# A hybrid decoder block on one core: the first transfers in another order and on other queues, and two output tiles that take the last merge tile's share at their end

## The chip, the cores and the metric

The kernel runs on one core of a Trainium2 chip. It is one launch of one program; the time is the device time of that core in microseconds (us), and the number that stands for a kernel is the median of its runs. All arithmetic is in float32: a factor that goes through the matrix engine is split into a high part (stored as fp32r) and a low part (what the high part leaves), and a product takes three matmuls: high by high, high by low, low by high.

## The reference

One layer over 512 positions and 1024 channels; eight heads of 64 in two key groups; a feed-forward width of 2816:

```python
h = rmsnorm(x, norm1_g)
a_b, a_c, a_x, q, kc, vc, ksl, vsl, kwn, vwn, g_nsa, g_merge = split(h @ w_in)
y_a = a_b * causal_dwconv(a_c * a_x, conv_a_w)
y_b = nsa(rope(rmsnorm(q)), k_cmp, v_cmp, k_sel, v_sel, k_win, v_win, sigmoid(g_nsa))
gm  = sigmoid(g_merge)
mix = gm[:, :D] * (y_a @ w_a_out) + gm[:, D:] * (y_b @ w_b_out)
x   = x + mix @ w_o
h   = rmsnorm(x, norm2_g)
gu  = h @ w_ffn_in
g   = causal_dwconv(gu[:, :D_FF], ffn_conv_w) + ffn_conv_b
x   = x + (silu(g) * gu[:, D_FF:]) @ w_ffn_out
```

## The kernel before, in words

Everything is held with channels on the 128 partitions, in KD = 8 channel tiles of 512 positions. The program is written stage by stage, but the order in which an engine gets its instructions is not the order of the text: a list scheduler with a simulated timeline places them (the context is opened with `schedule_with_timeline_sim=True`), so an edit in one place can move instructions in another. Each engine then works its own list strictly in order.

**The start.** `tok_round(0, first_slot)` makes the first projection: for each of eight channel tiles k, four position tiles (banks `pj_s`, three times, and `pj_o`) take three matmuls of 384 columns each: `xg_h` by `wh`, `xg_l` by `wh`, `xg_h` by `wl`. That is 12 matmuls per k and 96 in the round. `first_slot` is called for pairs of channel tiles, j = 0 to 3 (k = 0 and 1, 2 and 3, and so on). It issues the transfers (`par`, a table of 116 columns with the norm gains; `xT`, the input, into `x_all`; `w_tok`, the weights, into `wr_t`), then has ScalarE scale the input by the gain (L262, `xg_h`; VectorE makes `xg_l`, L263), split the weights (`split`, L152 and L153) and square the input for the norm's sums (L291). `chain(ops)` fixes the order of these on ScalarE. Ahead of it `NWU` = 11 matmuls on a tile of ones (`wu`, L183) keep the matrix engine busy while the first data arrive.

**The merge.** After the attention, the convolution branch and the gates, eight merge tiles are made, two per turn (L771 to L784): the matrix engine makes `pmb`, VectorE multiplies by the gate (L780), GpSimd adds the other branch (L781, `t_all`), ScalarE takes the high part (`mix_h`, L782), VectorE the low part (`mix_l`, L783).

**The output projection.** For the eight output tiles in `O_ORDER` = (0, 4, 1, 5, 2, 6, 3, 7): a weight tile is loaded (`ring_w`: raw tile, then high and low parts in rings of three), `dense` makes 24 matmuls into a bank `po` (16 with the high weights, 8 with the low ones; each pair of units needs one of the eight merge tiles, the last of them `mix_h[7]`, `mix_l[7]`), VectorE adds the input (L814), ScalarE makes `xv` and a square (L818, `sq`/`sqb`, L823), and after each second tile `x_forms` makes seven combinations of two halves (`xv`, L803 to L805) whose high and low parts `xf_h`, `xf_l` (L152 and L153, one step of 1792 columns per pair) feed the feed-forward part. All eight `po` banks come from the pool `d_bank`, which has two; `s_bank` has three, and the attention scores before and the feed-forward products `p45` and `p37` after it use that.

**The first feed-forward pair.** The products of pair 0 are written in two parts (`late`, L926 to L937): first three of the four channel units of every product (L931), then the last one (L937), since the last unit waits for the output projection's last pair. Between them stand the matmuls `pr_n` of the second norm's sums (L375).

Of the kernel before, what the change touches and what calls it, by code (L numbers as in the profile page):

```python
# [14 lines left out]
AF = mybir.ActivationFunctionType  # L15
# [5 lines left out]
S = 512  # L21
KD = D // P
# [23 lines left out]
NRAW = 4  # L46
NWF = 3
NE = 3
NWU = 11
QT_ORDER = (3, 2, 1, 0)  # L50
NPT = 3
NF_T = 10
# [30 lines left out]
def tile_block(ctx: ExitStack, tc: tile.TileContext, xT, pos, par, par2, w_tok, w_a3, w_gate, w_ao, w_bo, w_o,  # L83
               w_ff, w_dn, c_w1, out):
    nc = tc.nc
# [22 lines left out]
    def bank(tag, name, bufs):  # L108
        return ps.tile([P, 512], F32, name=name, tag=tag, bufs=bufs)

    def d_bank(name):
        return bank("d", name, 2)
# [53 lines left out]
    def raw_tile(name):  # L166
        return wf.tile([P, D], F32, name=f"wr_{name}", tag="wr", bufs=NRAW)

    def ring_w(src, name):
        raw = raw_tile(name)  # L170
        nc.sync.dma_start(raw, src)
        h, l = ring(name)
        split(h, l, raw)
        return h, l


    ones = const([P, P], "ones")
    nc.gpsimd.memset(ones, 1.0)
    warm = const([P, 2], "warm")
    nc.gpsimd.memset(warm[:, 1:2], 0.0)  # L180
    wu = d_bank("wu")
    for i in range(NWU):
        nc.tensor.matmul(wu[:, 0:P], ones, ones, start=True, stop=True)  # L183
    par_sb = const([P, NPAR], "par")
# [28 lines left out]
    def behind(later, earlier):  # L213

        tc.add_manual_dep(later.ins, earlier.ins.name,
                          mybir.DependencyInfo(mybir.DependencyClass.NoSync, mybir.DependencyReason.DATA),
                          reason="order")
# [51 lines left out]
    def first_slot(j, raw, hi, lo):  # L269
        a, b = CH[0]  # L270
        xr = x_all[:, 2 * j:2 * j + 2]
        if j == 0:
            nc.scalar.dma_start(par_sb, par)
            for k in range(2):
                nc.sync.dma_start(xr[:, k], xT[:, k])
                d = (nc.sync if k else nc.scalar).dma_start(raw[:, k], w_tok[k, :, a:b])
                if k == 0:

                    behind(nc.scalar.activation(warm[:, 0:1], ones[:, 0:1], AF.Copy), d)
            x0 = scale_x(0, xr[:, 0], (slice(0, S // 2), slice(S // 2, S)))  # L280
            w0 = split(hi[:, 0], lo[:, 0], raw[:, 0])
            x1 = scale_x(1, xr[:, 1], (slice(0, S),))
            w1 = split(hi[:, 1], lo[:, 1], raw[:, 1])
            ops = [x0[0], w0, x0[1]] + x1 + [w1]
        else:
            nc.sync.dma_start(xr, xT[:, 2 * j:2 * j + 2])
            nc.sync.dma_start(raw, w_tok[2 * j:2 * j + 2, :, a:b].rearrange("k p n -> p k n"))
            ops = [scale_x(2 * j + k, xr[:, k], (slice(0, S),))[0] for k in range(2)]
            ops.append(split(hi, lo, raw))
        sq = w_tmp(f"sq{j}", (2, S))  # L290
        ops.append(nc.scalar.activation(sq, xr, AF.Square))  # L291

        chain(ops)
        if j == 0:
            sq_sum.append(sq)
        else:
            nc.vector.tensor_add(sq_sum[0], sq_sum[0], sq)
# [102 lines left out]
    def dense(acc, units, first=True, last=True):  # L400

        for i, (wh, wl, xh, xl) in enumerate(units):
            nc.tensor.matmul(acc, wh, xh, start=first and i == 0, stop=False)  # L403
            nc.tensor.matmul(acc, wh, xl, start=False, stop=False)  # L404
        for i, (wh, wl, xh, xl) in enumerate(units):
            nc.tensor.matmul(acc, wl, xh, start=False, stop=last and i == len(units) - 1)  # L406

    def w_units(w, xh, xl, nk, k0=0, koff=0):
        wh, wl = w
        return [(wh[:, (koff + k) * P:(koff + k + 1) * P], wl[:, (koff + k) * P:(koff + k + 1) * P],  # L410
                 xh[:, k0 + k, :], xl[:, k0 + k, :]) for k in range(nk)]
# [357 lines left out]
    mix_h = const([P, KD, S], "mix_h", F32R, pc)  # L769
    mix_l = const([P, KD, S], "mix_l", F32R, pc)  # L770
    for i in range(4):  # L771
# [3 lines left out]
        w = ring_w(w_bo[i], f"bo{i}")  # L775
        for n, j in enumerate((2 * i, 2 * i + 1)):
            acc = t_bank(f"pmb{j}")
# [13 lines left out]
    x1 = const([P, KD, S], "x1", F32, px)  # L791
    O_ORDER = (0, 4, 1, 5, 2, 6, 3, 7)
# [13 lines left out]
        split(xf_h[:, k], xf_l[:, k], v)  # L806

    sq2 = sb.tile([P, S], F32, name="sq2", tag="rb")
    for n, j in enumerate(O_ORDER):
        w = ring_w(w_o[j], f"o{j}")  # L810
        acc = d_bank(f"po_{j}")
        dense(acc, w_units(w, mix_h, mix_l, KD))
        xj = x1[:, j, :]
        nc.vector.tensor_add(xj, xj, acc)  # L814
        k, half = j % 4, j // 4
        if half == 0:
            v = pc.tile([P, 7, TH], F32, name=f"xv{k}", tag="xv", bufs=2)
        nc.scalar.activation(v[:, 2 * half:2 * half + 2].rearrange("p a t -> p (a t)"), xj, AF.Copy,  # L818
                             scale=par_sb[:, G2 + j:G2 + j + 1])
        if half == 1:  # L820
            x_forms(k, v)
        sq = sq2 if n == 0 else pc.tile([P, S], F32, name=f"sqb{j}", tag="tb", bufs=2)
        nc.scalar.activation(sq, xj, AF.Square)  # L823
        if 0 < n < KD - 1:
            nc.vector.tensor_add(sq2, sq2, sq)
# [246 lines left out]
```

## Time and profile before

| what | value |
|---|---|
| median of the runs | 720.97 us |
| lowest run | 720.72 us |
| the profiled execution: its time, and its span from first to last instruction | 719.79 us, 718.1 us |
| matrix engine (PE) busy | 711.1 us, 99% of the span |
| VectorE (DVE), ScalarE (ACT), GpSimd (POOL) busy | 532.5, 437.7, 183.3 us |
| first matmul of the first projection | 6.36 us |
| the wait ahead of the output projection's last unit | 1.3 us |

How to read it: PE is the row of matmuls, PEld that of the weight loads that go beside them, and a name followed by q (SPq, ACTq, POOLq) is that engine's instruction queue issuing a transfer. A timeline row gives the start, the time taken, the engine, the line, the operation with the tiles it writes and reads, and in brackets how long the engine had been idle before it and what ended that. The buffer numbers are left out of the tiles' names. A row with a count, x2 or x8, is several instructions that follow each other, and its time is that of all. Matmuls are pipelined: a matmul's duration is longer than its distance to the next, and the distance is what counts.

### The profile page before, as it was taken

Reading aid. Unit: us, or ns where it says so; the run is one execution under the profiler, and the core shown is the slowest. Engines: PE = TensorE matmul, PEld = TensorE weight load, DVE = VectorE, ACT = ScalarE, POOL = GpSimd, SP = SyncE. Lnnn points to the kernel's source line nnn. Section 1 sums busy time; section 2 is a strip of 40 time slices with the busy share of each in tenths; the row PEclk is TensorE's granted clock in tenths of the full one; section 3 lists DMA queues with packets and bytes.
Section 4 is the critical chain, followed back from the end, with each engine's and each line's share of the span. In section 5 each row is a group of like instructions: output and inputs, shape, how many; then the busy total and the mean of one; then the engine's idle time right before and its main releaser. Section 6 shows DMA issues by size and latency. Waiting matters only on the chain.

```text
span 718.1 us, 11433 instructions
## 1 busy us (share of the span) xinstructions
PE 711.1 (99%) x4309; PEld 635.5 (89%) x4309; DVE 532.5 (74%) x973; ACT 437.7 (61%) x738; POOL 183.3 (26%) x176
## 2 busy tenths in 40 slices
PE   9999999999999999999999999999999999999997
PEld 8999888888888888887889999899999999999986
DVE  6887885677568676465695899997787877878643
ACT  7535655877667767443585776676564766646430
POOL 3151422133433333435011211221211222111110
PEclk9999999999999999999999999999999999999999
DMA  7333677511111221062676798987878778785575
GB/s 272 98 94 118 177 175 175 120 60 58 60 60 60 77 70 60 1 234 70 223 191 135 164 230 210 226 202 186 201 187 220 172 184 202 187 205 104 120 140 151
DMA packets 41143, 105.48 MB, mean 147 GB/s; under 512 B 3968, under 2 KB 9216, under 8 KB 41088
## 3 DMA queue, kind: packets, MB, share of 16 engines
q1 hardware_dynamic: 26528, 70.41, 29.8%
q0 software_dynamic: 14272, 34.08, 27.4%
q8 instruction: 34, 0.56, 0.3%
q10 hardware_dynamic: 288, 0.26, 0.1%
q14 instruction: 21, 0.17, 0.1%
HBM read 102.64 MB, written 2.10 MB: 146 GB/s over the span
## 4 chain that ended last, share of the span: by engine, by line
PE 96%; POOL 1%; DVE 1%; ACT 1%; DMA 1%; issue 0%; ACTq 0%
PE p L404 9%; PE p L406 9%; PE p L403 9%; PE pdn L404 6%; PE pdn L403 6%; PE pdn L406 6%; PE pg L403 4%; PE pg L404 4%; PE pg L406 4%; PE pa L403 3%; PE pa L406 3%; PE pa L404 3%; PE pt L650 2%; PE po L406 2%; PE po L403 2%; PE po L404 2%
## 5 line engine op out<-in xcount | busy, mean ns | idle before, releaser
L404 PE MATMUL p<-xf_l,sh 128*128 128x256 f32 x336 | 80.6, 277 | 0.0
L403 PE MATMUL p<-xf_h,sh 128*128 128x256 f32 x336 | 80.6, 277 | 0.0
L152 ACT ACTIVATE sh<-s 128x1024 fp32r<-128x1024 f32 x44 | 46.2, 1057 | 38.2 <-PE p L404 24.5
L404 PE MATMUL pdn<-al,wh_d 128*128 128x512 f32 x176 | 68.8, 391 | 0.0
L403 PE MATMUL pdn<-ah,wh_d 128*128 128x512 f32 x176 | 68.6, 391 | 0.0
L404 PEld LDWEIGHTS p<-xf_l,sh 128*128 128x128 f32 x336 | 63.0, 188 | 0.1
L403 PEld LDWEIGHTS p<-xf_h,sh 128*128 128x128 f32 x336 | 63.0, 188 | 0.1
L160 POOL DMA_DIRECT2D wl_s<-in_w_ff_dram x22 | 19.5, 885 | 167.6 <-ACT wl_s L159 156.1
L153 DVE TENSOR_TENSOR sl<-s,sh 128x1024 fp32r<-128x1024 f32 x44 | 53.8, 1225 | 8.7 <-ACT sh L152 8.7
L158 ACT ACTIVATE wh_s<-wr_s 128x1024 fp32r<-128x1024 f32 x22 | 23.3, 1057 | 53.5 <-PE pdn L404 50.1
L135 POOL TENSOR_TENSOR wl_g<-wr_g,wh_g 128x1024 fp32r<-128x1024 f32 x16 | 38.4, 2402 | 64.4 <-ACT wh_g L133 31.1
L406 PE MATMUL p<-xf_h,sl 128*128 128x256 f32 x336 | 51.6, 277 | 0.0
L403 PE MATMUL pg<-xg_h,wh_g 128*128 128x512 f32 x128 | 51.0, 398 | 0.0
L404 PE MATMUL pg<-xg_l,wh_g 128*128 128x512 f32 x128 | 50.7, 396 | 0.0
L406 PE MATMUL pdn<-ah,wl_d 128*128 128x512 f32 x176 | 47.7, 389 | 0.0
L160 POOL DMA_DIRECT2D wl_d<-in_w_dn_dram x22 | 26.5, 1203 | 77.6 <-ACT wl_d L159 70.4
L991 DVE TENSOR_TENSOR x<-x,pdn 128x512 f32<-128x512 f32 x48 | 33.1, 690 | 16.2 <-PE pdn L406 15.5
L406 PEld LDWEIGHTS p<-xf_h,sl 128*128 128x128 f32 x336 | 44.5, 188 | 0.2
L403 PE MATMUL p<-xf_h,wh_s 128*128 128x256 f32 x168 | 40.5, 277 | 0.0
L404 PE MATMUL p<-xf_l,wh_s 128*128 128x256 f32 x168 | 40.5, 277 | 0.0
L406 PEld LDWEIGHTS pdn<-ah,wl_d 128*128 128x128 f32 x176 | 33.0, 188 | 6.8
L404 PEld LDWEIGHTS pdn<-al,wh_d 128*128 128x128 f32 x176 | 33.1, 188 | 6.2
(348 smaller groups left out, 2138.4 us busy)
## 6 DMA issues: line engine op xcount, KB each, us to landing
wr_s<-in_w_ff_dram SPq DMA_DIRECT2D x44, 512.0 KB, 5.1
wl_s<-in_w_ff_dram POOLq DMA_DIRECT2D x22, 512.0 KB, 7.6
wr_d<-in_w_dn_dram SPq DMA_DIRECT2D x22, 512.0 KB, 6.5
wl_d<-in_w_dn_dram POOLq DMA_DIRECT2D x22, 512.0 KB, 8.5
wr_g<-in_w_gate_dram SPq DMA_DIRECT2D x16, 512.0 KB, 3.4
wr_a<-in_w_a_dram SPq DMA_DIRECT2D x12, 512.0 KB, 4.2
tl<-in_w_ff_dram POOLq DMA_DIRECT2D x22, 256.0 KB, 7.3
wl_a<-in_w_a_dram POOLq DMA_DIRECT2D x10, 512.0 KB, 7.5
```

Of the source, the lines that this page charges most:

```text
L135: e.tensor_sub(lo[:, 0:n], raw[:, 0:n], hi[:, 0:n].bitcast(F32))
L152: hi = nc.scalar.activation(h, v, AF.Copy)
L153: nc.vector.tensor_sub(l, v, h.bitcast(F32))
L158: nc.scalar.activation(h, raw, AF.Copy)
L160: nc.gpsimd.dma_start(l if dst is None else dst, src, accum_op=ALU.add)
L403: nc.tensor.matmul(acc, wh, xh, start=first and i == 0, stop=False)
L404: nc.tensor.matmul(acc, wh, xl, start=False, stop=False)
L406: nc.tensor.matmul(acc, wl, xh, start=False, stop=last and i == len(units) - 1)
L650: nc.tensor.transpose(pt[:, i * P:(i + 1) * P], e[:, i, kt * P:(kt + 1) * P], ident)
L991: nc.vector.tensor_add(xj, xj, acc)
```

## The change

It has two parts.

In `first_slot`, for the first pair, ScalarE's queue now issues the token weights of k = 0 alone. SyncE's queue issues the first half of the input's channel tile 0, then `par`, then the second half, then channel tile 1, then the weights of k = 1. On ScalarE the split of the weights now stands ahead of both scalings. There are 9 instead of 11 matmuls on ones.

In the output projection, a new function `open_o` loads the weights of the first two tiles (0 and 4), writes for each all matmuls with the first seven merge tiles (high and low weights), and after both the ones with the eighth merge tile. `dense` is called with `last=False` and `first=False` for the two pieces, so that both add to one bank. The third, fourth, seventh and eighth tiles take a bank of `s_bank`.

```diff
-NWU = 11
+NWU = 9
...
         if j == 0:
-            nc.scalar.dma_start(par_sb, par)
-            for k in range(2):
-                nc.sync.dma_start(xr[:, k], xT[:, k])
-                d = (nc.sync if k else nc.scalar).dma_start(raw[:, k], w_tok[k, :, a:b])
-                if k == 0:
-
-                    behind(nc.scalar.activation(warm[:, 0:1], ones[:, 0:1], AF.Copy), d)
+            d = nc.scalar.dma_start(raw[:, 0], w_tok[0, :, a:b])
+
+            behind(nc.scalar.activation(warm[:, 0:1], ones[:, 0:1], AF.Copy), d)
+            nc.sync.dma_start(xr[:, 0, 0:S // 2], xT[:, 0, 0:S // 2])
+            nc.sync.dma_start(par_sb, par)
+            nc.sync.dma_start(xr[:, 0, S // 2:], xT[:, 0, S // 2:])
+            nc.sync.dma_start(xr[:, 1], xT[:, 1])
+            nc.sync.dma_start(raw[:, 1], w_tok[1, :, a:b])
             x0 = scale_x(0, xr[:, 0], (slice(0, S // 2), slice(S // 2, S)))
             w0 = split(hi[:, 0], lo[:, 0], raw[:, 0])
             x1 = scale_x(1, xr[:, 1], (slice(0, S),))
             w1 = split(hi[:, 1], lo[:, 1], raw[:, 1])
-            ops = [x0[0], w0, x0[1]] + x1 + [w1]
+            ops = [w0, x0[0], x0[1]] + x1 + [w1]
...
+    first_o = {}
+
+    def open_o():
+
+        units = {}
+        for j in O_ORDER[0:2]:
+            units[j] = w_units(ring_w(w_o[j], f"o{j}"), mix_h, mix_l, KD)
+            first_o[j] = d_bank(f"po_{j}")
+            dense(first_o[j], units[j][0:KD - 1], last=False)
+        for j in O_ORDER[0:2]:
+            dense(first_o[j], units[j][KD - 1:], first=False)
+
+    open_o()
     for n, j in enumerate(O_ORDER):
-        w = ring_w(w_o[j], f"o{j}")
-        acc = d_bank(f"po_{j}")
-        dense(acc, w_units(w, mix_h, mix_l, KD))
+        acc = first_o.get(j)
+        if acc is None:
+            w = ring_w(w_o[j], f"o{j}")
+            acc = (s_bank if n % 4 > 1 else d_bank)(f"po_{j}")
+            dense(acc, w_units(w, mix_h, mix_l, KD))
```

How the instructions then stand is shown at three places. The first is the head of SyncE's list, before:

```order
L275 DMA x_all<-in_xT_dram 128x512 x2
L276 DMA wr_t_112<-in_w_tok_dram 128x384
L286 DMA x_all<-in_xT_dram 128x1024
L287 DMA wr_t_157<-in_w_tok_dram 128x2x384
L286 DMA x_all<-in_xT_dram 128x1024
```

and now:

```order
L276 DMA x_all<-in_xT_dram 128x256
L277 DMA par<-in_par_dram 128x116
L278 DMA x_all<-in_xT_dram 128x256
L279 DMA x_all<-in_xT_dram 128x512
L280 DMA wr_t_110<-in_w_tok_dram 128x384
L287 DMA x_all<-in_xT_dram 128x1024
L288 DMA wr_t_156<-in_w_tok_dram 128x2x384
```

The transfers of the second pair (128x1024, then 128x2x384) stood fourth and fifth on SyncE's queue and now stand sixth and seventh; on ScalarE's queue the weights were second, behind `par`, and are now first and alone.

The second place is the matrix engine's list at the end of the merge, from the low parts of the last merge tile's weights on. Before (`po_0` and `po_4` are the two first output tiles, `po_1` the third):

```order
L404 MATMUL po_0_3547<-mix_l_3159,wh_o0_3543 128x512
L404 MATMUL po_4_3582<-mix_l_3159,wh_o4_3578 128x512
L403 MATMUL po_0_3547<-mix_h_3158,wh_o0_3543 128x512
L403 MATMUL po_4_3582<-mix_h_3158,wh_o4_3578 128x512
L404 MATMUL po_0_3547<-mix_l_3159,wh_o0_3543 128x512
L406 MATMUL po_0_3547<-mix_h_3158,wl_o0_3544 128x512 x8
L404 MATMUL po_4_3582<-mix_l_3159,wh_o4_3578 128x512
L406 MATMUL po_4_3582<-mix_h_3158,wl_o4_3579 128x512 x8
L403 MATMUL po_1_3623<-mix_h_3158,wh_o1_3619 128x512
```

and now, from the same matmul on:

```order
L405 MATMUL po_0_3546<-mix_l_3158,wh_o0_3542 128x512
L407 MATMUL po_0_3546<-mix_h_3157,wl_o0_3543 128x512 x7
L405 MATMUL po_4_3574<-mix_l_3158,wh_o4_3570 128x512
L407 MATMUL po_4_3574<-mix_h_3157,wl_o4_3571 128x512 x7
L404 MATMUL po_1_3622<-mix_h_3157,wh_o1_3618 128x512
L405 MATMUL po_1_3622<-mix_l_3158,wh_o1_3618 128x512
L404 MATMUL po_1_3622<-mix_h_3157,wh_o1_3618 128x512
L405 MATMUL po_1_3622<-mix_l_3158,wh_o1_3618 128x512
L404 MATMUL po_1_3622<-mix_h_3157,wh_o1_3618 128x512
L404 MATMUL po_0_3546<-mix_h_3157,wh_o0_3542 128x512
L404 MATMUL po_4_3574<-mix_h_3157,wh_o4_3570 128x512
```

The two matmuls `po_0` and `po_4` with the last merge tile's high part stood right behind the row with the first seven tiles' last work; now 14 matmuls with low weights, one more of `po_4`, and five of `po_1` stand ahead of them.

The third place is ScalarE's list around the end of the output projection, where the scheduler moved instructions that the text of the change does not touch. Before (`sqb7` is the square of the last output tile, `xf_h` from `xv2` and `xv3` are the high parts that the third and fourth channel units need):

```order
L818 ACTIVATE xv3_3805<-x1_3523,par_86 128x512
L823 ACTIVATE sqb3_3807<-x1_3523 128x512
L158 ACTIVATE wh_s0_2_4153<-wr_s0_20_4144 128x1024
L152 ACTIVATE xf_h_3532<-xv2_3727 128x1792
L159 ACTIVATE wl_s0_2_4154<-wr_s0_20_4144 128x1024
L818 ACTIVATE xv3_3805<-x1_3523,par_86 128x512
L823 ACTIVATE sqb7_3848<-x1_3523 128x512
L152 ACTIVATE xf_h_3532<-xv3_3805 128x1792
```

and now:

```order
L158 ACTIVATE wh_s0_2_4152<-wr_s0_20_4143 128x1024
L834 ACTIVATE xv3_3804<-x1_3522,par_84 128x512
L839 ACTIVATE sqb3_3806<-x1_3522 128x512
L159 ACTIVATE wl_s0_2_4153<-wr_s0_20_4143 128x1024
L834 ACTIVATE xv3_3804<-x1_3522,par_84 128x512
L839 ACTIVATE sqb7_3847<-x1_3522 128x512
L152 ACTIVATE xf_h_3531<-xv2_3726 128x1792
L152 ACTIVATE xf_h_3531<-xv3_3804 128x1792
```

The weight step `wh_s0_2` went ahead of the seventh output tile's two steps, and the high part from `xv2` went behind the square of the last tile. On the matrix engine, seven products of pair 0 (L931) that stood between the sixth, seventh and eighth output tiles now stand behind the eighth.

## The prediction

> **What bounds the kernel now.** I read the page's busy times first, then the waits of the matrix engine (PE: matmuls; PEld: weight loads), then the timeline where a wait is long.
>
> ```profile
> PE 711.1 (99%) x4309; PEld 635.5 (89%) x4309; DVE 532.5 (74%) x973; ACT 437.7 (61%) x738; POOL 183.3 (26%) x176
> PE po L403 <- ACT mix_h L782: 1.3, 1, 1.3
> PE pj_s L253 <- ACT wh_t L152: 0.7, 1, 0.7
> PEld po L403 <- DVE x L814: 0.2, 1, 0.2
> ```
>
> Matmuls fill 99% of the span, so only what lies between them can be won. The named waits of useful matmuls are 1.3 us ahead of the output projection's last unit, 0.7 us ahead of the first projection, and a 0.2 us wait of a weight load for a bank. The change works on all three. It removes no useful matmul: the sum is one of waits, against the profiled execution's 719.79 us (span 718.1), which lies 1.2 under the median of 720.97; I carry the difference over to the median.
>
> **The merge.** This timeline stands around the longest wait:
>
> ```profile
> 339.23 0.61 PE L404 MATMUL po<-mix_l,wh_o 128*128 128x512 f32 x2
> 340.45 0.63 ACT L782 ACTIVATE mix_h<-t_all 128x512 fp32r<-128x512 f32 x1 [2.67 <-POOL t_all L781]
> 341.11 0.69 DVE L783 SCALAR_TENSOR_TENSOR mix_l<-t_all,mix_h 128x512 fp32r<-128x512 f32 x1 [1.83 <-ACT mix_h L782]
> 341.13 0.74 PE L403 MATMUL po<-mix_h,wh_o 128*128 128x512 f32 x2 [1.28 <-ACT mix_h L782]
> 341.86 0.51 PE L404 MATMUL po<-mix_l,wh_o 128*128 128x512 f32 x1
> 342.20 2.00 PE L406 MATMUL po<-mix_h,wl_o 128*128 128x512 f32 x8
> 344.27 1.98 PE L406 MATMUL po<-mix_h,wl_o 128*128 128x512 f32 x8
> 346.08 0.48 PE L403 MATMUL po<-mix_h,wh_o 128*128 128x512 f32 x1
> ```
>
> The last two rows give the pace: eight matmuls from 344.27 to 346.08 are 0.226 us each. The pair at 339.23 would let the next start at 339.68. Three more stand before the eight at 342.20; without a wait those eight would have begun at 339.68 + 3 x 0.226 = 340.36. So 1.84 us are lost: more than the 1.28 in brackets, since behind `mix_h` the third matmul waits for `mix_l` too, and the restart is slow.
>
> Now 20 matmuls stand between the pair's second one (339.46) and the last unit's first: seven low ones of `po_0`, of which the first takes the place at 339.68, one and seven of `po_4`, five of `po_1`. They last 20 x 0.226 = 4.5 us, to 344.2; `mix_h` is there at 341.08 and `mix_l` at 341.80. Both waits go, with 2 us to spare. The third tile's bank no longer waits for VectorE: another 0.1 of the 0.2 above, because the matmul itself started on its pace at 346.08. **The term is -1.9 us**, between -1.3 (the bracket alone) and -2.1 (with the whole bank wait).
>
> What is later next: the high weights of the fourth tile wait on ScalarE until `po_0` no longer reads its ring buffer. That was here:
>
> ```profile
> 342.40 1.06 ACT L152 ACTIVATE wh_o<-wr_o 128x1024 fp32r<-128x1024 f32 x1 [1.32 <-PE po L404]
> ```
>
> Now the last such read is the 25th matmul after 339.46, so ScalarE starts near 345.3 and ends at 346.4, while the fourth tile begins 1.9 us before its old time of 346.08 + 24 x 0.226 = 351.5, at 349.6. The low part is needed 16 matmuls later. That costs nothing; if this cover of 3.2 us were gone, each later us would be a us on PE.
>
> **The start.** The transfers' issues, from issue to landing, and the first steps on ScalarE:
>
> ```profile
> 0.80 0.40 ACTq L273 DMA_DIRECT2D par<-in_par_dram  x1
> 1.23 0.46 ACTq L276 DMA_DIRECT2D wr_t<-in_w_tok_dram  x1
> 2.18 0.43 SPq L286 DMA_DIRECT2D x_all<-in_xT_dram  x1
> x_all<-in_xT_dram SPq DMA_DIRECT2D x1, 256.0 KB, 3.7
> par<-in_par_dram ACTq DMA_DIRECT2D x1, 58.0 KB, 3.9
> wr_t<-in_w_tok_dram ACTq DMA_DIRECT2D x1, 192.0 KB, 4.5
> x_all<-in_xT_dram SPq DMA_DIRECT2D x1, 512.0 KB, 6.1
> 3.00:4.00 1.00, 1.00 (x7) 1.00 (x7) 0.00 (x0) 0.21 (x2) 0.93 (x2) 1.00 0.95 286
> 5.78 0.52 ACT L152 ACTIVATE wh_t<-wr_t 128x384 fp32r<-128x384 f32 x1 [0.53 <-DMA wr_t<-in_w_tok_dram]
> 6.21 1.11 ACT L262 ACTIVATE xg_h<-x_all,par 128x256 fp32r<-128x256 f32 x2
> 6.36 0.44 PE L253 MATMUL pj_s<-wh_t,xg_h 128*128 128x384 f32 x1 [0.72 <-ACT wh_t L152]
> 8.59 1.32 ACT L262 ACTIVATE xg_h<-x_all,par 128x512 fp32r<-128x512 f32 x2
> 9.81 0.83 ACT L152 ACTIVATE wh_t<-wr_t 128x768 fp32r<-128x768 f32 x1
> 10.69 0.19 PEld L253 LDWEIGHTS pj_s<-wh_t,xg_h 128*128 128x128 f32 x1 [0.23 <-ACT wh_t L152]
> ```
>
> Weights issued at 1.23 landed after 4.5, at 5.73. Issued at 0.80 (where `par` stood) they land between 0.80 + 3.7 = 4.5 (the first input transfer's time) and 0.80 + 4.5 = 5.3; I take 4.6, since they now share the engines with half a tile. The split then ends near 5.1. The first scaling, which was over before the split, now comes behind it and behind `par`, second on SyncE's queue: 0.80 + 0.43 for the issue ahead + 3.9 = 5.1. It ends near 5.65, so PE starts about 0.7 us earlier, at 5.7 instead of 6.36.
>
> That is not the gain. At 10.69 PE waited 0.23 us for the weights of k = 2: its next stop is ScalarE's chain, whose link is the second input transfer (512 KB), issued at 2.18, landed at 8.3, used at 8.59. From its use to PE's start of k = 2 are 10.69 - 8.59 = 2.1 us. With the split at 4.6 instead of 5.78 and one scaling of 0.5 more, ScalarE would be free for it 0.7 us earlier, at 7.9, but the transfer bounds it: two more issues of 0.43 us now stand ahead of it on SyncE's queue. If the bytes in front of it set its landing (the same bytes as before, and the engines 95% busy from 3 us on), it lands at 8.3 and 0.3 us is won; if the issue sets it, 0.86 us later, at 9.15, and 0.55 is lost. I take 8.5: **-0.1 us**, from -0.3 to +0.55. Below -0.3 it cannot go while that landing holds. Past k = 2 the round has cover.
>
> The Trainium skill, "Trainium Kernel Development and Optimization", Key Constraints, says that transfers issued from several engines' queues run on the same 16 DMA engines and interleave, so that another queue saves the issue time alone. The busy row above agrees; by the rule, nothing but the landing order changes, the second pair lands no earlier, and this term would be at best the 0.3.
>
> **The end of the output projection.** Here the scheduler moved work:
>
> ```profile
> 378.11 1.06 ACT L158 ACTIVATE wh_s<-wr_s 128x1024 fp32r<-128x1024 f32 x1 [0.95 <-PE po L404]
> 379.07 1.69 ACT L152 ACTIVATE xf_h<-xv 128x1792 fp32r<-128x1792 f32 x1
> 379.92 0.69 DVE L814 TENSOR_TENSOR x<-x,po 128x512 f32<-128x512 f32 x1 [1.62 <-PE po L406]
> 380.79 2.03 DVE L153 TENSOR_TENSOR xf_l<-xv,xf_h 128x1792 fp32r<-128x1792 f32 x1 [0.19 <-ACT xf_h L152]
> 381.61 0.70 ACT L818 ACTIVATE xv<-x,par 128x512 f32<-128x512 f32 x1
> 382.22 0.62 ACT L823 ACTIVATE sqb<-x 128x512 f32<-128x512 f32 x1
> 383.74 1.46 PE pr_n L375 x14
> 385.05 0.36 PE L931 MATMUL p<-xf_l,sh 128*128 128x256 f32 x1
> 385.19 4.24 PE p L931 x35
> ```
>
> (The rows at 383.74 and 385.19 are from the chain of waits: 14 norm passes, two to a matmul, and 35 products.) The row at 379.92 sets E, the end of the last output tile, at 379.9. The third unit's low part was ready at 382.82, and PE read it first at 385.05: 2.2 us of cover. In the new order ScalarE, from the release at E - 1.8 (378.11), does the weight step (1.0), the seventh tile's two steps (1.3), the low weight copy (1.0), the last tile's two steps (1.3) and only then this high part (1.7): E + 4.5, and VectorE's 2.0 us on top give E + 6.5; with the shorter distances between starts (0.96, 0.61, 0.55, 1.6), E + 6.2. PE has, from E - 0.2, 32 products at 0.12, eight norm matmuls at 0.21 and six products with the high part: 3.9 + 1.7 + 0.7, until E + 6.1. **So 0.1 to 0.4 us is lost; I take +0.3**, from 0 to +0.9 (if VectorE is busy with another step when the high part comes). Seven of the 32 products were done before E, and come out even.
>
> Further moves in the feed-forward part I cost at nothing: its matmuls show no wait above, and the lists agree again from the sixth pair on. Two matmuls fewer on ones are off the path while PE waits for data anyway.
>
> **Sum**: -1.9 - 0.1 + 0.3 = -1.7: 718.1 us for the profiled execution, 719.3 for the median.
>
> **The rivals.** *The second pair lands late*: +0.55 at the start instead of -0.1, which gives 719.9. For it speaks that two more issues stand ahead of it on its queue; against it the busy DMA engines. *The wait only changes its name*: the last unit's wait goes, but the fourth tile's weights, released by a matmul that now comes 2.5 us later, hold PE up as long: 721.0. Against it stands the cover of 3.2 us. *Slower, by the clock of the first matmuls*:
>
> ```profile
> 4.42 0.55 PEld L183 LDWEIGHTS wu<-ones 128*128 128x128 f32 x2
> 4.64 0.47 PEld L183 LDWEIGHTS wu<-ones 128*128 128x128 f32 x2
> 5.14 0.30 PEld L183 LDWEIGHTS wu<-ones 128*128 128x128 f32 x2
> 1.06 4.58 PE L183 MATMUL wu<-ones 128*128 128x128 f32 x22 [1.06 <-POOL ones L178]
> ```
>
> The granted clock reads 1.00 (the column after the engines' in the row at 3.00), yet two weight loads of these matmuls on ones took 0.55 us at 4.42 and 0.30 at 5.14: the pace rose near 5.0, 3.9 us after the first. Nine matmuls are 18 of the 22 passes; at 0.22 from start to start (4.42 to 4.64) they end at about 4.9 to 5.0, just as it rises. If it does not rise, the first projection runs at half pace from 5.7 on. If that lasts x us, x/2 is lost, of which the early start and the old 0.23 us wait take up 0.9. The other terms are worth -1.6, so from x = 5 the kernel is slower than before; with two stretches as long as the first 3.9 us, x is 7.8, the balance 3.9 - 0.9 - 1.6 = +1.4, and the time 722.4.
>
> The Trainium skill, "TensorE: Matmul & The Clock Gate", Part 1, has a gate that doubles the clock after a busy window of about 3.4 us, free-running against the kernel's start. By that rule 18 passes hold a whole window in fewer phases than 22 did, which is where this rival's chance comes from; this trace agrees with the doubling, and its 3.9 us from 1.06 to 5.0 fit a window.
>
> **Chances.** Forecast 0.66; late second pair 0.12; wait renamed 0.08; clock 0.06; the rest, 0.08, is for waits in the moved feed-forward order and for runs that differ more than these. The forecast's own bounds are -1.9 - 0.3 + 0 and -1.3 - 0.1 + 0.9, so 718.8 to 720.5; with the late pair and half a microsecond for the profile's distance from the median, 718.1 to 721.0. About 2% (14 us) is what a measurement of this kernel tells from no change, and no case reaches it: within 2% 0.98, and 0.01 for each side.
>
> **What would show it.** At the merge, no PE wait for `mix_h` and the last unit some 4.5 us behind the seventh: right. At the start, a first matmul near 5.7 and a wait of about 0.5 to 0.9 us at k = 2: right; no such wait would mean that the second pair landed earlier than I think, and a first round at 0.35 us a matmul would be the clock. At the end, a PE wait for `xf_l` under 0.9 us. A PE wait longer than 1 us anywhere in the output projection or the first feed-forward pairs would make the prediction wrong.

## The result, and the profile after

The changed kernel took 729.59 us (728.39 to 730.23) beside 720.97 us for the kernel before on the same chip: a ratio of 1.0112, with a 95% interval of 1.0093 to 1.013. (One execution of the kernel before, of 1447.38 us, is left out of its median.) By the ratio the change costs 8.1 us where a gain of 1.7 was forecast; that is under 2%, but well clear of the noise, and the median lies 8.6 us above the forecast's upper end. The profiled execution took 730.23 us, 10.4 more than the profiled one of before.

The page of the changed kernel, and its waits of PE (in total, times, longest):

```profile
PE 716.2 (98%) x4305; PEld 639.8 (88%) x4305; DVE 534.0 (73%) x973; ACT 438.2 (60%) x738; POOL 186.2 (26%) x176
PE p L407 <- DMA wl_s<-in_w_ff_dram: 4.6, 1, 4.6
PE p L947 <- DVE xf_l L153: 1.2, 1, 1.2
PE pj_s L253 <- ACT wh_t L152: 0.5, 1, 0.5
PE pa L407 <- DMA wl_a<-in_w_a_dram: 0.5, 1, 0.5
```

PE's wait for `mix_h` is gone, as forecast. Two waits are new, for `wl_s` in the feed-forward part and for `xf_l` at the end of the output projection. They don't make up 10.4 us by themselves. PE is busy 5.1 us longer with the same useful work, so that some of it ran slower. The granted clock (the share of its full rate that the profile records for PE) had a mean of 1.000 before and has 0.992 now: it reads 0.5, called half clock below, from 385.32 to 392.15 us, beginning in the wait for `xf_l`, and from 457.00 to 460.41, behind the wait for `wl_s`.

**The merge** did what was forecast. The timeline of PE:

```profile
341.01 1.75 PE L407 MATMUL po<-mix_h,wl_o 128*128 128x512 f32 x7
342.82 1.75 PE L407 MATMUL po<-mix_h,wl_o 128*128 128x512 f32 x7
344.41 0.39 PE L404 MATMUL po<-mix_h,wh_o 128*128 128x512 f32 x1
```

The matmuls follow each other at 0.227 us with nothing between them. PE is 1.55 us later than before at the last `mix_l` matmul ahead of the rows above (340.78, before 339.23), and 0.44 us earlier at the first matmul of the fourth tile (351.21, before 351.65), so that 1.9 to 2.0 us are won between.

**The start.** ScalarE's timeline, one issue of SyncE's queue, and PE at k = 2:

```profile
3.13 0.51 SPq L287 DMA_DIRECT2D x_all<-in_xT_dram  x1
6.98 0.73 ACT L262 ACTIVATE xg_h<-x_all,par 128x512 fp32r<-128x512 f32 x1 [0.92 <-DMA x_all<-in_xT_dram]
10.20 0.83 ACT L152 ACTIVATE wh_t<-wr_t 128x768 fp32r<-128x768 f32 x1
11.07 0.45 PE L253 MATMUL pj_s<-wh_t,xg_h 128*128 128x384 f32 x1 [0.54 <-ACT wh_t L152]
```

The second pair's input is issued at 3.13 instead of 2.18, but it isn't what ScalarE waits for. It waits 0.92 us, until 6.98, for the input of k = 1, which is issued fourth on the queue now. Everything behind that on ScalarE comes later, and k = 2 starts at 11.07 us instead of 10.70.

**The end of the output projection** (PE's last matmuls for it, VectorE, ScalarE, then PE again):

```profile
376.60 1.98 PE L407 MATMUL po<-mix_h,wl_o 128*128 128x512 f32 x8
379.73 0.69 DVE L911 TENSOR_TENSOR s<-wr_s,wr_s 128x512 f32<-128x512 f32 x1 [0.90 <-DMA wr_s<-in_w_ff_dram]
380.34 0.68 DVE L830 TENSOR_TENSOR x<-x,po 128x512 f32<-128x512 f32 x1
382.20 1.68 ACT L152 ACTIVATE xf_h<-xv 128x1792 fp32r<-128x1792 f32 x1
384.00 2.02 DVE L153 TENSOR_TENSOR xf_l<-xv,xf_h 128x1792 fp32r<-128x1792 f32 x1
386.07 0.58 PE L947 MATMUL p<-xf_l,sh 128*128 128x256 f32 x1 [1.17 <-DVE xf_l L153]
386.45 0.41 PE L947 MATMUL p<-xf_h,sl 128*128 128x256 f32 x1
```

The last output tile ended near 378.6. VectorE could add it only at 380.34, because an earlier step of its list (`s<-wr_s`) waited for a transfer. From there the order of the steps is the one forecast. PE waits 1.17 us, and then the products follow at 0.21 us (from 386.45 on, to the next at 386.67) instead of 0.12, since the clock is at half.

**The fourth pair of chunks** (f = 6; its first weights are `wl_s0_6`) brings the larger wait. First ScalarE, GpSimd and PE in the changed kernel:

```profile
441.75 1.04 ACT L158 ACTIVATE wh_s<-wr_s 128x1024 fp32r<-128x1024 f32 x1
446.54 0.63 ACT L158 ACTIVATE th<-wr_s 128x512 fp32r<-128x512 f32 x1 [3.74 <-DMA wr_s<-in_w_ff_dram]
447.60 1.04 ACT L159 ACTIVATE wl_s<-wr_s 128x1024 fp32r<-128x1024 f32 x1
448.94 0.85 POOL L160 DMA_DIRECT2D wl_s<-in_w_ff_dram  x1
456.56 0.88 PE L407 MATMUL p<-xf_h,wl_s 128*128 128x256 f32 x4 [4.56 <-DMA wl_s<-in_w_ff_dram]
457.44 0.42 PE L405 MATMUL p<-xf_l,wh_s 128*128 128x256 f32 x1
```

And the same steps in the kernel before, with the row that tells the landing of the transfer issued at 438.89:

```profile
437.55 1.05 ACT L159 ACTIVATE wl_s<-wr_s 128x1024 fp32r<-128x1024 f32 x1
438.89 0.85 POOL L160 DMA_DIRECT2D wl_s<-in_w_ff_dram  x1 [6.67 <-ACT wl_s L159]
440.68 0.63 ACT L158 ACTIVATE th<-wr_s 128x512 fp32r<-128x512 f32 x1 [1.04 <-DMA wr_s<-in_w_ff_dram]
447.85 0.64 PE L406 MATMUL p<-xf_h,wl_s 128*128 128x256 f32 x4
wl_s<-in_w_ff_dram POOLq DMA_DIRECT2D x1, 512.0 KB, 5.7
```

Before, ScalarE made `wl_s` right behind `wh_s` (436.60 to 437.55), GpSimd issued the low weights' transfer at 438.89, it landed 5.7 us later, at 444.6, and PE read the weights at 447.85. In the new list two passes on the second weights, `th` and `tl`, stand between `wh_s` and `wl_s`. They wait 3.74 us for their transfer, and `wl_s`, which waits for nothing, waits behind them. The low weights are issued at 448.94, and PE has them only 7.6 us later.

Where the 10.4 us of the profiled executions are, by the shift of PE's start times against before, in the order of the program:

| stage | shift, us |
|---|---|
| start, at k = 2 | +0.4 |
| convolutions, waits for the low weights `wl_a` | +1.15 |
| merge | -1.9 |
| end of the projection: wait for `xf_l`, then slow products | +4.4 |
| fourth pair: wait for `wl_s` | +4.7 |
| fourth pair: slow products behind it | +1.7 |

### The profile page after: what moved, and what is told of

Read it like the earlier page. It is cut to its first block, busy times and chain, and to the rows that moved or that the text cites. A ratio compares the mean times of both kernels' runs of the same rounds, so it can differ in the third digit from the quotient of the medians.

```text
span 728.5 us, 11432 instructions
## 1 busy us (share of the span) xinstructions
PE 716.2 (98%) x4305; PEld 639.8 (88%) x4305; DVE 534.0 (73%) x973; ACT 438.2 (60%) x738; POOL 186.2 (26%) x176
## 4 chain that ended last, share of the span: by engine, by line
PE 79%; DMA 7%; DVE 6%; ACT 3%; issue 3%; POOL 1%; SPq 1%; DVEq 0%; ACTq 0%; POOLq 0%
PE p L407 7%; PE p L405 7%; PE p L404 7%; PE pdn L405 5%; PE pdn L404 5%; PE pdn L407 5%; PE pg L404 4%; PE pg L405 4%; PE pg L407 4%; DMA wr_s<-in_w_ff_dram 4%; PE pa L404 2%; PE pt L651 2%; PE pa L405 2%; PE pa L407 2%; PE sc L598 1%
```

## Experiments

Theory A was: the split wins its 1.9 us; the start loses about 1; the new banks made the scheduler move instructions, which gave the wait for `wl_s`, and the clock of PE (TensorE in the expectations) falls to half behind the new waits. The rivals are named in each expectation; in the first four, rival C is that the shifted start makes later transfers land badly.

The diffs of the first, second, fourth, fifth, seventh and ninth run are against the changed kernel, the others against what is named.

**The start alone** (the changed kernel with the old projection; `open_o` and `first_o` go too):

```diff
     for n, j in enumerate(O_ORDER):
-        acc = first_o.get(j)
-        if acc is None:
-            w = ring_w(w_o[j], f"o{j}")
-            ...
+        w = ring_w(w_o[j], f"o{j}")
+        acc = d_bank(f"po_{j}")
+        dense(acc, w_units(w, mix_h, mix_l, KD))
```

> The kernel before with the start's edit alone (first transfers, order on ScalarE, 9 matmuls on ones). Theory A (what costs 10 us is the order that the scheduler made of the output projection and the feed-forward part): only the start's own share shows, +0.4 us at the third channel tile, and up to +1.2 us more if the convolution's waits for low weights come with it: 721.6 to 722.8. Rival C (a shift of the start makes later transfers fall badly): 726 to 730, with the waits at 385 and 452 us in its trace.

It took 721.59 us beside 720.57, a ratio of 1.0015 (1.0005 to 1.0025). The new start loses, by about 1 us, as theory A has it. Its waits of PE:

```profile
PE pa L407 <- DMA wl_a<-in_w_a_dram: 1.7, 1, 1.7
PE po L404 <- ACT mix_h L783: 1.3, 1, 1.3
PE pj_s L253 <- ACT wh_t L152: 0.9, 1, 0.9
```

The first matmul came at 5.04 us, 1.3 earlier than before, and k = 2 at 11.30, 0.6 later. ScalarE waits 1.05 us for the input of k = 1 here, and then 0.41 us, until 9.18, for the second pair's input too. The wait for `wl_a` is a second share of the loss, and it differs between executions (none to 1.9 us in the profiles here). What sets the landing of `wl_a` stays open.

**The split of the two tiles, all accumulators in d banks** (and the old start):

```diff
-            acc = (s_bank if n % 4 > 1 else d_bank)(f"po_{j}")
+            acc = d_bank(f"po_{j}")
```

> The kernel before with the split of the two first output tiles, but with all eight output tiles in the old pool of two banks; the start is the old one. Theory A: ScalarE's and GpSimd's lists are then those of before, so nothing is late: the wait of 1.84 us at the merge goes, 719.2 to 719.5, no wait for xf_l or wl_s, no half clock. Rival B (the split itself delays the weights behind it): 724 or more.

720.38 us, a ratio of 1.0001 (0.9992 to 1.0011): a miss. The expected gain was not there, and the profile says why:

```profile
PE po L403 <- DVE x L829: 1.4, 1, 1.4
```

The wait only changed its name. Both first tiles now end late, so that both d banks are given back late by VectorE's additions (L829), and the third tile waits for one.

**The split with the s banks of the change, the old start:** the changed output projection whole, against the run above.

```diff
-            acc = d_bank(f"po_{j}")
+            acc = (s_bank if n % 4 > 1 else d_bank)(f"po_{j}")
```

> The kernel before with the whole output projection edit (split and the second pool), and the old start. Theory A: the lists of ScalarE and GpSimd are those of the changed kernel from the output projection on, so it has both waits (1.2 us for xf_l and 4.6 us for wl_s of the fourth pair) and both stretches at half clock: 727 to 729. Rival C: 719 to 720.

726.33 us, a ratio of 1.0078 (1.0063 to 1.0093). Nearly all of the loss belongs to this part of the change, though a little less than expected (727 to 729 us): PE waits 4.1 us for `wl_s` and then has 6.8 us of half clock, but at the end of the projection there is neither a wait over 0.2 us nor half clock.

**The whole change, but all accumulators in d banks:**

```diff
-            acc = (s_bank if n % 4 > 1 else d_bank)(f"po_{j}")
+            acc = d_bank(f"po_{j}")
```

> The changed kernel with all eight output tiles in the old pool of two banks. Theory A: e1 and e2 add up: 719.7 to 721.0. Rival B: 726 or more; rival C: 726 or more.

721.19 us, a ratio of 1.001 (1.0 to 1.002). The choice of the bank, in one line, thus stands between this and the 1.0112 of the whole change. PE waits 1.7 us for the third tile's bank here too, and the start loses 0.8 us against the same kernel with the old one.

**The split with one s bank, the third tile's, and the old start:**

```diff
-            acc = (s_bank if n % 4 > 1 else d_bank)(f"po_{j}")
+            acc = (s_bank if n == 2 else d_bank)(f"po_{j}")
```

> The kernel before with the two-tile split at the end of the merge, and one accumulator, the third tile's, in an s bank; all others stay in d banks, the start is the old one. Theory A (the split is worth the 1.9 us wait for mix_h as long as the third tile doesn't have to wait for a d bank, and the late s banks of the changed kernel are what brought the feed-forward waits): no TensorE wait for mix_h, none over 0.5 us for x, none for wl_s in the sixth and later weights, granted clock 1.0 throughout, time 718.4 to 719.2 us, 0.996 to 0.998 of the kernel before. Rival B (the 1.9 us always come back, as they did when both banks stayed d: the work behind the merge is bounded by something else than TensorE, so the wait turns up at another tile): 720.0 to 721.0 us with a new wait of 1 to 2 us in the output projection. Rival C (any s bank in the output projection shifts the feed-forward order): 724 us or more, with a wait for wl_s.

718.69 us beside 720.46, a ratio of 0.998 (0.9964 to 0.9996). Its two waits of PE for useful work, with none left in the projection and none in the feed-forward part:

```profile
PE pa L406 <- DMA wl_a<-in_w_a_dram: 0.3, 1, 0.3
PE ph L457 <- ACT qT L567: 0.3, 1, 0.3
```

The split is worth 1.4 to 1.8 us once the third tile has a bank. Rivals B and C fall: no wait of 1 to 2 us came back, and none for `wl_s` came up.

**The s banks of the change and the old start (the third run), with ScalarE's old order in the fourth pair:**

```diff
-        ff_pair(f, 1, up, ff_forms(f, 1))
+        form1 = ff_forms(f, 1)
+        if f == 6:
+            for act in form1["ends"]:
+                behind(act, form["last"])
+        ff_pair(f, 1, up, form1)
```

Here `ends` are the passes `th` and `tl` of the second weights and `last` is the pass `wl_s` of the first; `behind` places its first argument behind its second in the list. Nothing else moves in the lists of ScalarE, VectorE, GpSimd and SyncE against the third run, but for GpSimd's two transfers that follow these passes.

> The split with five s banks and the old start, which took 726.33 us, with one thing added: in the feed-forward part's fourth pair of chunks ScalarE must make the pass wl_s of the first weights ahead of the passes th and tl of the second weights, as it did in the kernel before. Theory A (the 4.1 us wait for wl_s comes from that order alone: the pass was queued behind two passes whose transfer had not landed, and the half clock of 6.8 us behind it comes from the wait): no wait for wl_s over 0.5 us, no half clock, 718.5 to 720.0 us. Rival B (the wait is for the transfer itself, which the queues bring late in this kernel whatever the order of the passes): the wait stays at 3 to 4 us and the time at 725 to 726.5 us. Rival C (the order is the cause of the wait, but the half clock comes from the five s banks): 721.5 to 723 us with half clock and no wait.

719.48 us, a ratio of 0.9997 (0.9979 to 1.0014), against 1.0078 without that order: 0.8% or 5.8 us come from three instructions' order. ScalarE and GpSimd there:

```profile
438.80 1.04 ACT L158 ACTIVATE wh_s<-wr_s 128x1024 fp32r<-128x1024 f32 x1
439.75 1.04 ACT L159 ACTIVATE wl_s<-wr_s 128x1024 fp32r<-128x1024 f32 x1
442.79 0.64 ACT L158 ACTIVATE th<-wr_s 128x512 fp32r<-128x512 f32 x1 [2.00 <-DMA wr_s<-in_w_ff_dram]
441.08 0.90 POOL L160 DMA_DIRECT2D wl_s<-in_w_ff_dram  x1 [7.14 <-ACT wl_s L159]
```

The second weights are late here too, but now only `th` and `tl` stand behind them. PE's wait and the half clock are gone from the profile. Theory A stands. The median is 0.8 us above that of the kernel with one s bank; the intervals of the two overlap, and no run shows what the other moves in the projection cost.

**The changed kernel with wide norm matmuls** (`wd` is 128 for the second norm, and 2 else; the lines that set and read it are left out):

```diff
-                sums = nc.tensor.matmul(pr[:, 2 * t:2 * t + 2], v[:, t * P:(t + 1) * P], ones[:, 0:2],
+                sums = nc.tensor.matmul(pr[:, wd * t:wd * t + wd], v[:, t * P:(t + 1) * P], ones[:, 0:wd],
```

> The changed kernel with one size changed: the eight norm matmuls at the end of the output projection have a moving operand of 128 columns in place of 2 (columns of ones, the result is the same in every column); they stand at the same place in the list. TensorE's wait for xf_l and the wait for wl_s are otherwise as they were. Theory A (the granted clock fell to half at the end of the projection because the stretch before it held 1.8 us of two-column matmuls and then a wait of 1.2 us, so that the array was little used): no half clock behind the xf_l wait, the passes there go on at 0.12 us, 725.5 to 726.8 us; the half clock behind the wait for wl_s stays. Rival B (any wait of a microsecond at this place halves the clock, whatever runs before it): half clock for 6.8 us as before, 729 to 731 us. Rival C (the wider matmuls only push the rest back): half clock gone, but 0.8 us more of matmuls behind the wait, 726.5 to 728 us.

726.96 us (724.93 to 730.59), a ratio of 1.0079 (1.0056 to 1.0101). There is no half clock at the end of the projection in its profile and the median is close to theory A's range, but the run doesn't decide: in the profile, of the slowest of four executions, PE does not wait for `xf_l` at all, so that the cause that rival B names was gone too. The wide matmuls took no more time than those of two columns (0.22 us from one to the next).

**Another start:** the kernel before, with the weights ahead of the parameters on ScalarE's queue.

```diff
-            nc.scalar.dma_start(par_sb, par)
+            d = nc.scalar.dma_start(raw[:, 0], w_tok[0, :, a:b])
+            nc.scalar.dma_start(par_sb, par)
...
-            ops = [x0[0], w0, x0[1]] + x1 + [w1]
+            ops = [w0, x0[0], x0[1]] + x1 + [w1]
```

> The kernel before with another start: ScalarE's queue issues the token weights ahead of the parameters and ScalarE splits the weights first, as in the change, but the parameters stay on ScalarE's queue and SyncE's list is untouched (whole inputs, no halves, eleven filler matmuls). Theory A (the changed start lost because SyncE had two more transfers to issue, 0.47 us each, so that the input of k=1 and the second pair landed later and ScalarE, with its squares behind them, reached the second pair's weights 0.4 to 0.6 us later): here ScalarE does not wait for k=1, the first matmul of k=2 comes at 10.1 to 10.5 us in place of 10.7, and the time is 0.2 to 0.6 us lower, 720.0 to 720.4 us, unless the waits for wl_a in the convolutions take it back. Rival B (weights ahead of the parameters is what loses, since the first scaling waits for the parameters): k=2 at 11.0 us or later, 720.8 to 721.6 us. Rival C (the start is absorbed by the waits for wl_a whichever way it moves): k=2 earlier by 0.3 us or more, but 720.5 to 721.5 us.

720.78 us, a ratio of 1.0001 (0.9992 to 1.001), with k = 2 at 10.71. None of the three fits. ScalarE's rows:

```profile
4.89 0.52 ACT L152 ACTIVATE wh_t<-wr_t 128x384 fp32r<-128x384 f32 x1 [1.67 <-DMA wr_t<-in_w_tok_dram]
5.81 1.52 ACT L262 ACTIVATE xg_h<-x_all,par 128x256 fp32r<-128x256 f32 x3 [0.40 <-DMA par<-in_par_dram]
```

ScalarE does not wait for k = 1, and this much is as theory A has it: with SyncE's list untouched that input lands in time. But the weights land at 4.9 here, not at 4.1 as in the changed kernel, and the parameters at 5.8. The wait moves from the weights to the parameters, and the chain behind is where it was. That the extra issues on SyncE's queue cost the changed start its 0.4 to 0.6 us agrees with this run, but only by contrast; no run took them away alone.

**The changed kernel with ScalarE's old order in the fourth pair:** the edit of the sixth run, in the changed kernel.

> The changed kernel, 729.59 us, with one thing added: in the fourth pair of chunks ScalarE must make the pass wl_s of the first weights ahead of the passes th and tl of the second ones, as before the change. In the changed kernel's profile the wait for wl_s was 4.7 us and the half clock behind it lasted 3.4 us, of which about 1.5 us were lost. Theory A (that order is the cause of both, and the rest of the loss is the start and the wait for xf_l with its half clock): no wait for wl_s, one half clock of 6.8 us at most, 722.8 to 724.2 us. Rival B (what is left of the changed kernel depends on when its transfers land, so that the wait for xf_l comes and goes): no wait for wl_s, and 719.5 to 722.5 us. Rival C (the wait moves to the next weights): 726 us or more.

721.42 us, a ratio of 1.0017 (1.0002 to 1.0031). The order takes 0.95%, or 6.8 us, off the changed kernel. Again, against the changed kernel, only `wl_s` and the two transfers change places in the lists. Theory A had left the wait for `xf_l` with its half clock in; rival B's range holds it:

```profile
PE pa L408 <- DMA wl_a<-in_w_a_dram: 1.8, 1, 1.8
PE p L405 <- ACT sh L152: 1.2, 1, 1.2
PE p L948 <- DVE xf_l L153: 0.6, 1, 0.6
```

The wait for `xf_l` is 0.6 us here, with the clock at 1.00. The instructions up to there are those of the changed kernel, so that this part of its loss hangs on when its transfers land, not on the lists alone. So does the wait of 1.2 us for `sh`, earlier in the feed-forward part: ScalarE waits 2.37 us there for weights, and 0.72 in the changed kernel's profile, with the same list. Three of the ten executions (722.58, 722.82 and 725.04 us) had a mean clock of 0.995 to 0.997, so that half clock came up in some of them; no trace shows where.

**Narrow matmuls alone:** work added behind the last matmul of the kernel with one s bank; its results are not used.

```diff
+    tail = s_bank("tail")
+    ops = [at_end[-1]]
+    ops += [nc.tensor.matmul(tail[:, 0:2], ones, ones[:, 0:2], start=True, stop=True) for _ in range(64)]
+    ops += [nc.tensor.matmul(tail[:, P:2 * P], ones, ones, start=True, stop=True) for _ in range(60)]
+    chain(ops)
```

> The kernel with the split and one s bank, which took 718.69 us, with work added behind its last matmul: 64 matmuls of 128 by 128 with 2 moving columns one after the other, and then 60 with 128 moving columns, in a bank that nothing reads. TensorE waits for nothing in them. At full clock they take about 64 times 0.11 and 60 times 0.195, 7.2 and 11.7 us. Theory A (a stretch of 3.41 us that is filled with two-column matmuls counts as little used, and the granted clock falls to half for what follows, as it did behind the eight norm matmuls and the short wait): a record of half clock that begins 3.4 to 6.9 us behind the first narrow matmul, and wide ones of 0.38 to 0.40 us until it ends. Rival B (the clock falls for waiting alone): clock 1.0 until the last wide matmul, all of them at 0.19 to 0.21 us.

Two rows of PE's timeline, and four stretches (length, busy time of each engine with its instructions, granted clock, DMA share, GB/s):

```profile
713.75 22.95 PE L1027 MATMUL tail<-ones 128*128 128x2 f32 x124
736.56 16.07 PE L1028 MATMUL tail<-ones 128*128 128x128 f32 x120
...
714.34:717.76 3.42, 3.42 (x32) 3.42 (x33) 0.00 (x0) 0.00 (x0) 0.00 (x0) 1.00 0.23 91
717.76:721.17 3.41, 3.41 (x18) 3.41 (x18) 0.00 (x0) 0.00 (x0) 0.00 (x0) 0.50 0.00 0
738.24:741.65 3.41, 3.41 (x18) 3.41 (x18) 0.00 (x0) 0.00 (x0) 0.00 (x0) 0.50 0.00 0
741.65:745.06 3.41, 3.41 (x32) 3.41 (x32) 0.00 (x0) 0.00 (x0) 0.00 (x0) 1.00 0.00 0
```

PE never waits, and yet the clock is at half from 717.76 us on, after 3.41 us with nothing but two-column matmuls. It stays there through all of them and comes back at 741.65, 5.1 us into the wide ones. Theory A stands, rival B falls. The durations were mis-sized: a matmul is two passes in these rows (128 for the 64 narrow ones, of which the row shown leaves out the first four, from 713.39 us on), each of 0.107 us at full clock and 0.19 at half, where the expectation had taken a whole matmul of two columns at 0.11 us and of 128 at 0.195.

## Why the prediction was wrong

*The merge, -1.9 us*: right in size and in mechanism. The fourth tile's weights were begun at 346.88 us, forecast 345.3 and 1.55 for the later start of this stretch, and held nothing up. The rival that the wait only changes its name was placed at these weights. It is real at another place, the third tile's bank, and the s bank of the change is what keeps it away: with d banks it took the whole gain back, with one s bank the gain was measured.

*"Further moves in the feed-forward part I cost at nothing"*: this is the step that failed, and it made 5.8 to 6.8 of the 8.1 us that the ratio gives (sixth and ninth run, in which ScalarE's old order takes the loss away). Both reasons given for it were poor. "Its matmuls show no wait above" says nothing of the cover, and the cover could be read in the trace of before: low weights issued at 438.89, landed at 444.6, read at 447.85, so 3.3 us are spare. And the lists that "agree again from the sixth pair on" differ in the fourth, where `wl_s` went behind two passes that in the trace of before already waited 1.04 us for their transfer, until 440.68. By an estimate from these rows, behind them and at their own pace of 0.53 us each, `wl_s` would have been made from 441.74 to 442.8 and been issued near 443; with 5.7 us of landing as before, or 7.6 as in the changed kernel, it would have come 0.9 to 2.8 us late. The 4.7 us measured are more, since the second weights landed 5.9 us later than before, at 446.5, while PE was 4.0 us later; why they landed that late stays open. The prediction gave waits in this part, together with everything else, a chance of 0.08, without a price. With the order put right (ninth run) the change still costs 1.2 us (0.1 to 2.2), so that this step is most of the miss and not all of it.

*The end of the output projection, +0.3, to +0.9*: too small in the profiled execution, where it was +4.4. The order of the steps and PE's time there were right: PE was forecast at E + 6.1 and got there at about E + 6.3. `xf_l` came at E + 7.4 instead of E + 6.2, because the step that adds the last tile began 1.8 us behind E, after VectorE's wait for `wr_s`. The forecast had let that step start at once, as in the row of before. Then 6.8 us of half clock followed, which nothing in the forecast provided for. Without the start's edit (third run), and again in the seventh and ninth, that wait was 0.6 us or less and the clock stayed up, so that the forecast's 0 to +0.9 covers the waits that were seen where the half clock did not follow. Which of the late transfer, the wait and the narrow norm matmuls it takes for the half clock here was argued from the clock's records below, not tested on its own at this place. The half clock at this place was not shown to belong to the change in each of its executions.

*The start, -0.1, from -0.3 to +0.55*: the sign was wrong. It measured +0.4 us at k = 2 in the changed kernel's profile and +0.2 to +0.6 in the four others with this start, mostly at the far end of the range, and about 1 us in time with what the convolutions add. The forecast followed the second pair's input, while ScalarE waited for the input of k = 1, 0.9 to 1.8 us in all five profiles; only in the run of the start alone did the second pair bind too, by 0.41 us. The sign that was to show the forecast right, a wait of 0.5 to 0.9 us at k = 2, was met with 0.54 us, but by another transfer and with a first matmul at 5.09 instead of 5.7, so that it proved nothing. By the rule that the Trainium skill, "Trainium Kernel Development and Optimization", Key Constraints, states, that issues from several queues run on the same 16 DMA engines, the forecast held -0.3 to be the best this part could bring. No run of a start beat that.

*The rival of the first matmuls' clock*: it came to pass in small. The clock rose at 6.44 us, 1.35 us after the first matmul at 5.09, and the wait at k = 2 took that up; it cost nothing that can be seen. Nor does it belong to the nine matmuls alone: in the profiles with the old start and eleven of them, the clock first rose anywhere from 4.37 to 7.25 us, twice 0.6 to 1.1 us behind the first matmul. *The sign* that was to make the prediction wrong, a PE wait over 1 us there, was met, by `xf_l` in the first pair and by `wl_s` in the fourth.

## What to carry to other kernels

Where a scheduler sets the lists, compare every engine's list to the end of the program, and for each transfer that moved take from the old trace the time between its issue and its first reader less the time it needs to land. A buffer's choice is such a move: here one word for a bank's pool sent a pass that waits for nothing behind two that wait, far from the change. A stall of PE is not to be priced by its length alone: behind the wait of 1.2 us here some 3 us more were lost at half clock, and behind the one of 4.6 us another 1.7.

## What the runs showed of the clock

The granted-clock records of two profiled executions, in us from the first instruction, with the length and that length divided by 3.4133 us (of the second only the first three; the last record of each, behind the last matmul, is left out):

```
changed kernel       start    length   clock  length / 3.4133
                       6.44    378.88   1.0    111.0
                     385.32      6.83   0.5      2.0
                     392.15     64.85   1.0     19.0
                     457.00      3.41   0.5      1.0
                     460.41    266.24   1.0     78.0
wide norm matmuls      7.17     75.09   1.0     22.0
                      82.26      3.41   0.5      1.0
                      85.68    368.64   1.0    108.0
```

So the clock changes only at the borders of stretches of 3.413 us, which are counted from wherever it first rose. (Ahead of the first record the profile's rows give 1.00, though the changed kernel's first three matmuls, at 5.09, took 1.60 us and three of k = 1, at 8.16, took 0.79.) The stretches ahead of a fall and behind it, first in the changed kernel (the second figure is PE's busy time, the third from the end the clock):

```profile
381.91:385.32 3.41, 3.00 (x26) 2.79 (x24) 3.34 (x6) 3.12 (x3) 0.00 (x0) 1.00 1.08 221
385.32:388.73 3.41, 2.66 (x12) 2.66 (x13) 2.70 (x3) 0.55 (x1) 2.56 (x1) 0.50 0.36 70
388.73:392.15 3.42, 3.42 (x18) 3.42 (x17) 0.69 (x1) 0.00 (x0) 0.18 (x1) 0.50 0.02 5
453.59:457.00 3.41, 0.44 (x3) 0.45 (x4) 3.41 (x7) 1.43 (x2) 1.19 (x1) 1.00 0.94 261
```

Then one stretch of the kernel with wide norm matmuls, with a fall behind it:

```profile
78.85:82.26 3.41, 1.55 (x10) 1.14 (x10) 2.85 (x6) 2.61 (x7) 0.00 (x0) 1.00 0.56 174
```

And one of the kernel with the new start alone, with none behind it:

```profile
80.14:83.55 3.41, 1.69 (x10) 1.23 (x9) 3.01 (x9) 2.80 (x7) 0.03 (x1) 1.00 0.49 167
```

Waits of 1.9 and 1.7 us at the same place differ in what follows, and PE was busy 1.55 us of the one stretch and 1.69 of the other. In all profiles here, between the first rise and the last matmul, a full-clock stretch with 1.55 us or less, 45%, was followed by half clock, and one with 1.69 or more, 50%, was not, with two exceptions, and both hold two-column matmuls: the stretch of the last experiment that holds nothing else, and the one at 381.91, whose 3.00 us are 1.76 us of such matmuls and 1.24 of others. So by these two such matmuls count for little. At half clock, a stretch with 2.66 us, in the second row, did not bring the clock back, and one with 3.42 did, though 3.41 us of two-column matmuls did not; no run shows a stretch between. Where in the count a wait falls matters too: waits of 4.1 and 4.4 us for `wl_s` (third and seventh run) were followed by two stretches at half clock, the one of 4.6 us in the changed kernel by one. That the same wait could cost half clock in one execution and nothing in the next would follow, but no run shows it. The Trainium skill, "TensorE: Matmul & The Clock Gate", Part 1, states such a free-running window of 3413 ns, and the records agree with it. Its table under "Why this matters for your kernels" advises against idle gaps over about 3 us; here a wait of 1.9 us was enough, and matmuls with no gap at all were.
